# A Mamba-2 layer with a convolutional MLP: second norm's sums moved into the output projection, a chunk's own part added by TensorE, two buffers for a chunk's factors, context tiles transposed one by one

## The chip, the cores and the metric

The kernel runs on one core of a Trainium2 chip. The metric is the device time of one execution in microseconds. A core has TensorE (PE in the profile; PEld is its weight load), VectorE (DVE), ScalarE (ACT), GpSimd (POOL) and SyncE (SP). Each takes its instructions in a fixed order; in this kernel SP does nothing but issue DMAs.

## The reference

The model is one layer: a bidirectional Mamba-2 mixer and then a gated convolutional MLP, on 512 latent tokens of 1024 channels with 256 context tokens in front. Everything is float32.

```python
sh1, sc1, g1, sh2, sc2, g2 = split(silu(c) @ ada_w + ada_b, 6)     # modulation
hc, hl = modulate(rmsnorm(ctx)), modulate(rmsnorm(x))
z, xbc, dt = split(h @ w_in)                  # for context and latent tokens
xs, b, c = split(silu(conv1d(xbc, 3 taps)))   # 32 heads of 64, 4 groups, state of 128
# per direction, chunks of 128 tokens; the latent scan starts from the context's last state
y = (c b^T * decay) (dt xs)  +  decay_from_start * (c state)
x = x + g1 * (rmsnorm((y + d * xs) * silu(z)) @ w_out)
a, g = split(modulate(rmsnorm(x), sh2, sc2) @ w_up)
x = x + g2 * ((silu(conv2d(a, 3x3)) * g) @ w_down)
return rmsnorm(x)
```

## The kernel before

Products that must be exact to float32 are made of three passes: a weight tile is split into a rounded `hi` (ACT) and a rest `lo` (DVE or POOL), the activations too, and PE adds hi·hi, lo·hi and hi·lo. A raw weight tile of 512 KB comes through the pool `wraw` (three slots, line 84) and becomes a pair of the pool `wsp` (three slots, line 85). Small products, transposes and sums over partitions run on PE in plain float32.

The stages are: (1) modulation of the first norm, norm, first columns of the input projection; (2) `dt_path` (line 523), the decay factors of all heads, mostly on DVE, whose results go to DRAM (`da_d`, `em_d`, `e_d`) to be read back spread over partitions; (3) four groups of eight heads: `proj_pieces(g)` (638) projects the group's columns b, x0 to x3 and c, each with a 3-tap convolution (`conv_silu`, 629), and `ssm_group(g)` (714) runs its recurrence; (4) `gate_pieces` (822), 16 columns of z; (5) the output projection with the second norm; (6) up projection with the 3x3 convolution; (7) down projection and last norm.

`ssm_group` goes through four chunks. `mixing(ch)` (753) loads a chunk's factors: `R` (one buffer, line 759) and `M` (two) and `eb` (one). DVE scans `R` in place, adds its two directions into `M`, and multiplies `M` by `cb`. PE then makes `pi`, the chunk's own part, from `M` and the tokens `xk`, and `pe`, twice, from the states of either direction; DVE multiplies both by `eb`, adds the two, adds them to `pi`, and adds `pi` to `u` (lines 797 to 814). `pi` and both `pe` take a PSUM bank each from `py`, which has three. `advance` (745) carries a state on by one chunk. `context_states(g)` (676) transposes the context's b and x columns of the group once all five are projected, through the one bank of `pt`, and makes the first states.

The modulation's parts 2 (`g1`), 3 and 4 (second norm's shift and scale) are matrix by vector products that DVE makes: `ada_pieces` (843) loads a 512 KB tile of `ada_w` through `wraw` and adds its product with the column `s` to `ada_acc`, eight pieces per part. `ada_to_cols` (866) turns such a sum into columns with 16 small matmuls. `with_ada` (904) puts one such piece behind each piece of projection; as there are 24, they lie in the phases of groups 1 to 3 and the first gates. `blend` (931) emits the group's recurrence and after each of its eight steps so many pieces of the next phase as the ratio says (0.6, 0.6, 0.9, 0.6); the rest of the phase comes after it.

The order in which instructions are emitted is a priority. A scheduler in the compiler then sets each engine's order by its own estimate of times, except where `hold` or `T.held` pins the order to that of the program: in stage 1, and for PE from the last quarter of the output projection to the first columns of the up projection.

The output projection (`token_matmul`, 969, called at 1077) runs 16 tiles of `w_out` over four token tiles of two banks each. The first three and the last four tiles of weights are taken together, so that token tiles finish one after another; `add_and_norm` (1033) and `modulated` (1048) then make the input of the up projection in place of them, `h2hi` and `h2lo`. `gate2` (1101) makes part 5 in the up projection.

Of the kernel before, what the change touches and what calls it, by code (L numbers as in the profile page):

```python
# [10 lines left out]
F32 = mybir.dt.float32  # L11
F32R = mybir.dt.float32r
# [6 lines left out]
P = 128  # L19
# [47 lines left out]
def hybrid_kernel(  # L67
# [138 lines left out]
    gp = ph1.enter_context(tc.tile_pool(name="gp", bufs=2))  # L206
    ca = ph1.enter_context(tc.tile_pool(name="ca", bufs=1))

# [5 lines left out]
    def bank(pool, name):  # L214
        return pool.tile([P, 512], F32, tag=pool.name, name=name)
# [422 lines left out]
    def proj_pieces(g):  # L638

        def start():  # L640

            bT = gp.tile([P, LAT], F32, tag="bT", name=f"bT{g}", bufs=1)
            cT = gp.tile([P, LAT], F32, tag="cT", name=f"cT{g}")
            bTc = ca.tile([P, CTX], F32, tag="bTc", name=f"bTc{g}")
            xTc = ca.tile([P, 4, CTX], F32, tag="xTc", name=f"xTc{g}")
            grp[g] = bT, cT, bTc, xTc

        def run(raw, nm, m):
            if nm == "b":
                start()  # L650
            bT, cT, bTc, xTc = grp[g]
            if nm[0] == "x":
                i = int(nm[1])
                dl, dc = u[:, 4 * g + i], xTc[:, i]
            else:
                dl, dc = (bT, bTc) if nm == "b" else (cT, None)
            if raw is None:
                pl, pc = ps_first[nm]
            else:
                whi, wlo = split(raw, f"{nm}{g}", G if g == 0 or (g == 1 and nm in ("b", "x0", "x1", "x2")) else None)  # L660
                pc = dc is not None and project(whi, wlo, chi, clo, CTX, f"pc_{nm}{g}")
                pl = project(whi, wlo, hhi, hlo, LAT, f"pl_{nm}{g}", py if g == 0 else pj)
            if dc is not None:
                conv_silu(pc, m, CTX, dc, f"c{nm}{g}")
            conv_silu(pl, m, LAT, dl, f"l{nm}{g}")

        def finish(_):
            bT, cT, bTc, xTc = grp[g]
            grp[g] = bT, cT, context_states(g, bTc, xTc)

        for nm, m in [("b", 16 + g)] + [(f"x{i}", 4 * g + i) for i in range(4)] + [("c", 20 + g)]:
            load = partial(raw_cols, w_in, INNER + m * P, f"{nm}{g}")
            yield (None if g == 0 and nm in ps_first else load), partial(run, nm=nm, m=m)
        yield None, finish

    def context_states(g, bTc, xTc):
        bk = cx.tile([P, CTX], F32, tag="bkc", name=f"bkc{g}")
        tp = bank(pt, f"tbc{g}")
        for cc in range(2):
            T.transpose(tp[:, cc * P:(cc + 1) * P], bTc[:, cc * P:(cc + 1) * P], ident)  # L680
        A.copy(bk, tp[:, :CTX])
        S = [sp.tile([P, 512], F32, tag=f"S{dr}", name=f"S{dr}_{g}_0", bufs=(3, 4)[dr]) for dr in range(2)]
        xk = []
        for cc in range(2):
            tp = bank(pt, f"txc{g}{cc}")
            for i in range(4):
                T.transpose(tp[:, i * P:(i + 1) * P], xTc[:, i, cc * P:(cc + 1) * P], ident)
            t = cx.tile([P, 512], F32, tag=f"xkc{cc}", name=f"xkc{g}{cc}")
            A.copy(t, tp)
            xk.append(t)  # L690
        for dr in range(2):
            ps = bank(pst, f"sc{g}{dr}")
            for cc in range(2):
                local_state(ps, bk, cc, weighted(xk[cc], dr, 4 + cc, g), cc == 0, cc == 1)
            A.copy(S[dr], ps)
        return S
# [7 lines left out]
    def weighted(xk, dr, ch, g):  # L704
        t = cx.tile([P, 512], F32, tag="xw", name=f"xw{g}_{ch}_{dr}", bufs=2)
        G.tensor_tensor(
            heads(t), heads(xk),
            ej(tokcol(tok_w, dr, ch, g)), op=ALU.mult)
        return t
# [4 lines left out]
    def ssm_group(g):  # L714
# [38 lines left out]
        def mixing(ch):  # L753
# [4 lines left out]
            M = sp.tile([P, HPG, 2, BL], F32, tag="M", name=f"M{g}{ch}", bufs=2)  # L758
            R = sp.tile([P, 2, HPG, BL], F32, tag="R", name=f"R{g}{ch}", bufs=1)
            halves = [(b, slice(BL * b, BL * b + BL)) for b in range(2)]  # L760
# [36 lines left out]
        for ch in range(NC):  # L797
            cs = slice(ch * P, (ch + 1) * P)
            M, eb = nxt
            pi = bank(py, f"pi{g}{ch}").rearrange("p (j l) -> p j l", l=P)  # L800
            for j in range(4):
                for q in range(2):
                    h = 2 * j + q
                    mm(pi[64 * q:64 * q + 64, j], xk[:, ch, h * HD:(h + 1) * HD], M[:, 4 * q + j])
            t = eb
            for dr, S in ((0, Sf), (1, Sb[ch])):
                pe = bank(py, f"pe{g}{ch}{dr}").rearrange("p (j l) -> p j l", l=P)
                for j in range(4):
                    mm(pe[:, j], S[:, j * P:(j + 1) * P], cT[:, cs])
                V.tensor_tensor(pe if dr else t[:, 0], pe, eb[:, dr], op=ALU.mult)  # L810

            V.tensor_tensor(t[:, 0], t[:, 0], pe, op=ALU.add)
            V.tensor_tensor(pi, pi, t[:, 0], op=ALU.add)
            us = u[:, 4 * g:4 * g + 4, cs]
# [50 lines left out]

    def ada_to_cols(part, a):
        pc = bank(pj, f"ada_c{part}")
        for m in range(KD):
# [9 lines left out]

    def ada_to_rows(a, name):
        parts = split(a, name)  # L880
        for h in range(2):
# [22 lines left out]
    def with_ada(pieces):  # L904
        for p_ in pieces:
            yield p_
            yield from islice(ada, 1)

    ada = chain(ada_pieces(3, ada_acc, then=ada_to_cols), ada_pieces(4, ada_acc, then=ada_to_cols),
                ada_pieces(2, ada_acc, then=ada_bias))  # L910
    phases = [proj_pieces(0)] + [with_ada(p_) for p_ in (
        proj_pieces(1), proj_pieces(2), chain(proj_pieces(3), gate_pieces(0)),
        chain(gate_pieces(1), gate_pieces(2)), gate_pieces(3))] + [ada]
    ends = []
# [31 lines left out]
    finish_phase(0)  # L946
    for g, ratio in enumerate((0.6, 0.6, 0.9, 0.6)):
        blend(ssm_group(g), g + 1, ratio)
# [16 lines left out]
    h2hi = x2p.tile([P, KD, LAT], F32R, tag="h2hi", name="h2hi")  # L965
    h2lo = x2p.tile([P, KD, LAT], F32R, tag="h2lo", name="h2lo")
    Q.dma_start(x2, x.rearrange("(i p) d -> p i d", p=P))
# [49 lines left out]
    with tc.tile_pool(name="uo", bufs=5) as uo, tc.tile_pool(name="wlo", bufs=4) as wlast:  # L1017
# [11 lines left out]
        last_of = lambda: [wlast.tile([P, 1024], F32R, tag=n, name=f"{n}_last") for n in ("whi", "wlo")]  # L1029
        get_w = lambda k, last: wrows(w_out, k, f"o{k}", None, last_of if last else None)  # L1030
        xns = {}
# [45 lines left out]
        for i, o in token_matmul(acc8, 16, get_w, get_u, 3, 4, 512, up_ahead):  # L1077
            add_and_norm(i, o)
            if 0 < i < 3:
                modulated(i - 1, acc8[i - 1])  # L1080
# [20 lines left out]
    def gate2():  # L1101
        yield from stream(ada_pieces(5, g2r, True, ada_bias), 0)
        ada_to_rows(g2r, "g2b")
        yield
# [111 lines left out]
```

## Time and profile before

| | us |
|---|---|
| three timed runs | 969.15, 971.22, 972.81 |
| median | 971.22 |
| profiled execution | 972.9 |
| its span on the core | 971.1 |

| engine | busy, us | share of the span |
|---|---|---|
| PE | 902.7 | 93% |
| DVE | 717.2 | 74% |
| ACT | 344.8 | 36% |
| POOL | 301.6 | 31% |

All instructions are issued through one helper, so the profile puts them all on line 59; they are told apart by the tile that they write, as `pi` or `ada_acc`. "A <- B" after a wait names what ended it. The granted clock is the share of 2.4 GHz that TensorE had in a stretch, and its two levels are 1.2 and 2.4 GHz.

### The profile page before, as it was taken

What the parts mean: (1) busy time and instruction counts of PE and PEld (TensorE: products, weight loads), DVE (VectorE), ACT (ScalarE), POOL (GpSimd) and SP (SyncE); (2) the same over time, 40 slices, a digit from 0 to 9 for tenths busy, and PEclk for the clock granted to TensorE, in tenths of its full rate; (3) what the DMA queues carried; (4) which work ended last, traced back from release to release, by engine and by line L of the source; (5) the groups of instructions that cost most, each with busy time, mean ns of one, the idle gap of its engine ahead of it and who ended that gap; (6) DMA issues with size and microseconds to landing.
All of it is one profiled execution on the core that took longest, in us unless ns stands there. A gap on an engine that the chain in (4) does not pass through costs nothing.

```text
span 971.1 us, 12065 instructions
## 1 busy us (share of the span) xinstructions
PE 902.7 (93%) x4595; PEld 736.8 (76%) x4595; DVE 717.2 (74%) x961; ACT 344.8 (36%) x523; POOL 301.6 (31%) x223
## 2 busy tenths in 40 slices
PE   7999868788889979899999999999989999999996
PEld 6688756666667767687888888888868888888885
DVE  5689989888977889657754457878898888843336
ACT  6463332222213322334344336444544333321223
POOL 2133249454535632414100004002400000453446
PEclk9999888899999999899999999999999999999998
DMA  9923364435554365533434350334534333323322
GB/s 313 292 57 101 109 145 119 112 94 155 169 144 120 98 184 141 141 88 104 135 121 140 109 152 1 112 112 148 161 107 120 87 107 92 105 87 92 104 65 87
DMA packets 137891, 119.70 MB, mean 123 GB/s; under 512 B 23245, under 2 KB 118249, under 8 KB 137833
## 3 DMA queue, kind: packets, MB, share of 16 engines
q1 hardware_dynamic: 137833, 118.93, 42.3%
q8 instruction: 36, 0.59, 0.3%
q14 instruction: 22, 0.18, 0.1%
HBM read 116.49 MB, written 2.43 MB: 122 GB/s over the span
## 4 chain that ended last, share of the span: by engine, by line
PE 51%; DVE 24%; DMA 12%; issue 9%; POOL 2%; ACT 2%; SPq 1%; DVEq 0%; ACTq 0%; POOLq 0%
PE d L59 12%; PE o L59 8%; PE pz L59 8%; PE pg L59 7%; PE pa L59 6%; DMA R<-da_d 5%; DMA adaw<-in_ada_w_dram 4%; DVE M L59 3%; DVE ada_acc L59 3%; DVE R L59 2%; DVE et L59 2%; PE pl_x L59 2%; DVE fc L59 2%; SPq L59 1%; DVE cv_lx L59 1%
## 5 line engine op out<-in xcount | busy, mean ns | idle before, releaser
L59 DVE SCALAR_TENSOR_TENSOR fc<-pa,prmC,fc 128x441 f32<-128x441 f32 (+2 forms) x176 | 121.4, 693 | 13.3 <-ACT fc L59 9.8
L59 POOL TENSOR_TENSOR raw_d<-raw_d,g2r 128x1024 f32<-128x1024 f32 x22 | 56.1, 2556 | 176.1 <-DMA raw_d<-in_ffn_w_down_dram 159.8
L59 PE MATMUL pa<-h2lo,hi_a 128*128 128x512 f32 (+1 forms) x192 | 71.5, 373 | 0.8 <-POOL h2lo L59 0.5
L59 PE MATMUL pa<-h2hi,lo_a 128*128 128x512 f32 (+1 forms) x192 | 71.5, 372 | 0.6 <-DVE lo_a L59 0.6
L59 PE MATMUL pa<-h2hi,hi_a 128*128 128x512 f32 (+1 forms) x192 | 71.5, 373 | 0.1
L59 PE MATMUL pg<-h2hi,lo_g 128*128 128x512 f32 (+1 forms) x184 | 70.1, 381 | 0.4 <-DVE lo_g L59 0.4
L59 PE MATMUL pg<-h2hi,hi_g 128*128 128x512 f32 (+1 forms) x184 | 70.1, 381 | 0.0
L59 PE MATMUL pg<-h2lo,hi_g 128*128 128x512 f32 (+1 forms) x184 | 69.9, 380 | 0.0
L59 DVE TENSOR_TENSOR lo_d<-raw_d,hi_d 128x1024 fp32r<-128x1024 f32 x18 | 34.2, 1902 | 42.9 <-ACT hi_d L59 42.9
L59 PE MATMUL pl_x<-hhi,hi_x 128*128 128x512 f32 x128 | 54.2, 425 | 4.0 <-DVE cv_cx L59 4.0
L59 POOL TENSOR_TENSOR M<-M,tok_m 64x512 f32<-64x512 f32 x32 | 41.9, 1310 | 51.1 <-DMA M<-em_d 43.2
L59 DVE TENSOR_TENSOR_SCAN R<-R,dg 128x1024 f32<-128x1024 f32 x16 | 40.2, 2516 | 23.7 <-DMA R<-da_d 17.2
L59 PE MATMUL pl_x<-hhi,lo_x 128*128 128x512 f32 x128 | 53.4, 419 | 0.0
L59 PE MATMUL pz<-hhi,lo_z 128*128 128x512 f32 x128 | 52.7, 412 | 0.0
L59 PE MATMUL pz<-hhi,hi_z 128*128 128x512 f32 x128 | 52.7, 412 | 0.0
L59 PE MATMUL pl_x<-hlo,hi_x 128*128 128x512 f32 x128 | 51.6, 405 | 0.0
L59 PE MATMUL pz<-hlo,hi_z 128*128 128x512 f32 x128 | 51.2, 400 | 0.0
L59 POOL TENSOR_TENSOR dg<-diag,tok_dt 128x1024 f32<-128x1024 f32 x16 | 34.4, 2148 | 42.7 <-DVE R L59 41.7
L59 POOL TENSOR_TENSOR xw<-xk,tok_w 128x512 f32<-128x512 f32 x24 | 35.1, 1468 | 34.1 <-PE ps_Sf L59 17.1
L59 PE MATMUL d<-lo_d,fhi 128*128 128x512 f32 x144 | 44.5, 389 | 0.0
L59 PE MATMUL d<-hi_d,flo 128*128 128x512 f32 x144 | 44.5, 389 | 0.0
L59 PE MATMUL d<-hi_d,fhi 128*128 128x512 f32 x144 | 43.6, 389 | 0.0
(339 smaller groups left out, 2410.6 us busy)
## 6 DMA issues: line engine op xcount, KB each, us to landing
adaw<-in_ada_w_dram SPq DMA_DIRECT2D x32, 512.0 KB, 3.8
raw_a<-in_ffn_w_up_dram SPq DMA_DIRECT2D x22, 512.0 KB, 4.6
raw_g<-in_ffn_w_up_dram SPq DMA_DIRECT2D x22, 512.0 KB, 4.0
raw_d<-in_ffn_w_down_dram SPq DMA_DIRECT2D x22, 512.0 KB, 3.7
adaw<-in_ada_w_dram SPq DMA_DIRECT2D x8, 1024.0 KB
raw_x<-in_ssm_w_in_dram SPq DMA_DIRECT2D x16, 512.0 KB, 3.9
R<-da_d SPq DMA_DIRECT2D x32, 256.0 KB, 4.4
eb<-e_d SPq DMA_DIRECT2D x32, 256.0 KB, 5.1
```

The lines of the kernel that those rows point to most:

```text
L59: ins = f(*a, **kw)
```

## The change

1. Parts 3 and 4 of the modulation are summed in the output projection: each `get_w` takes one tile of `w_out` and then one piece of these parts. They have their own accumulator `ada34`, which lies under the tag of `h2lo`. Their column sums follow the second token tile and use columns of a PSUM bank of the first; `h2lo` is allocated after that. Part 2 stays in front, now behind the gate pieces of groups 1 to 3. The last blend ratio is 1.2 instead of 0.6.
2. In a chunk `pe` of the forward direction comes first; DVE multiplies it by `eb` in its PSUM bank, and the matmuls of `pi` are accumulated on it there. The product of the backward direction is written over `eb`, and one DVE instruction adds it.
3. `R` has two buffers, `xw` three.
4. Each context column is transposed and copied as soon as it is projected, from a buffer of 256 columns (two of them); `context_states` is left with the products.
5. In `gate2` the split of `g2r` is emitted a step before its matmuls.

```diff
-    ca = ph1.enter_context(tc.tile_pool(name="ca", bufs=1))
+    ca = ph1.enter_context(tc.tile_pool(name="ca", bufs=2))
...
-            if dc is not None:
+            if dk is not None:
+                dc = ca.tile([P, CTX], F32, tag="xTc", name=f"xTc{nm}{g}")
                 conv_silu(pc, m, CTX, dc, f"c{nm}{g}")
+                tp = bank(pt, f"tc{nm}{g}")
+                for cc in range(2):
+                    T.transpose(tp[:, cc * P:(cc + 1) * P], dc[:, cc * P:(cc + 1) * P], ident)
+                A.copy(dk, tp[:, :CTX].rearrange("p (c n) -> p c n", n=P))
...
-        t = cx.tile([P, 512], F32, tag="xw", name=f"xw{g}_{ch}_{dr}", bufs=2)
+        t = cx.tile([P, 512], F32, tag="xw", name=f"xw{g}_{ch}_{dr}", bufs=3)
...
-            R = sp.tile([P, 2, HPG, BL], F32, tag="R", name=f"R{g}{ch}", bufs=1)
+            R = sp.tile([P, 2, HPG, BL], F32, tag="R", name=f"R{g}{ch}", bufs=2)
...
-            pi = bank(py, f"pi{g}{ch}").rearrange("p (j l) -> p j l", l=P)
+            pes = []
+            for dr, S in ((0, Sf), (1, Sb[ch])):
+                pe = bank(py, f"pe{g}{ch}{dr}").rearrange("p (j l) -> p j l", l=P)
+                for j in range(4):
+                    mm(pe[:, j], S[:, j * P:(j + 1) * P], cT[:, cs], start=(j == 0))
+                V.tensor_tensor(eb[:, 1] if dr else pe, pe, eb[:, dr], op=ALU.mult)
+                pes.append(pe)
+            pi = pes[0]
             for j in range(4):
                 for q in range(2):
                     h = 2 * j + q
-                    mm(pi[64 * q:64 * q + 64, j], xk[:, ch, h * HD:(h + 1) * HD], M[:, 4 * q + j])
-            t = eb
-            for dr, S in ((0, Sf), (1, Sb[ch])):
-                pe = bank(py, f"pe{g}{ch}{dr}").rearrange("p (j l) -> p j l", l=P)
-                for j in range(4):
-                    mm(pe[:, j], S[:, j * P:(j + 1) * P], cT[:, cs])
-                V.tensor_tensor(pe if dr else t[:, 0], pe, eb[:, dr], op=ALU.mult)
-
-            V.tensor_tensor(t[:, 0], t[:, 0], pe, op=ALU.add)
-            V.tensor_tensor(pi, pi, t[:, 0], op=ALU.add)
+                    mm(pi[64 * q:64 * q + 64, j], xk[:, ch, h * HD:(h + 1) * HD], M[:, 4 * q + j], start=False)
+            V.tensor_tensor(pi, pi, eb[:, 1], op=ALU.add)
...
-    ada = chain(ada_pieces(3, ada_acc, then=ada_to_cols), ada_pieces(4, ada_acc, then=ada_to_cols),
-                ada_pieces(2, ada_acc, then=ada_bias))
-    phases = [proj_pieces(0)] + [with_ada(p_) for p_ in (
-        proj_pieces(1), proj_pieces(2), chain(proj_pieces(3), gate_pieces(0)),
-        chain(gate_pieces(1), gate_pieces(2)), gate_pieces(3))] + [ada]
+    ada = ada_pieces(2, ada_acc, then=ada_bias)
+    phases = [proj_pieces(0), proj_pieces(1), proj_pieces(2), chain(proj_pieces(3), gate_pieces(0)),
+              with_ada(chain(gate_pieces(1), gate_pieces(2))), with_ada(gate_pieces(3)), ada]
...
-    for g, ratio in enumerate((0.6, 0.6, 0.9, 0.6)):
+    for g, ratio in enumerate((0.6, 0.6, 0.9, 1.2)):
...
-    h2lo = x2p.tile([P, KD, LAT], F32R, tag="h2lo", name="h2lo")
+    ada34 = x2p.tile([P, 4, D], F32, tag="h2lo", name="ada34")
...
-        get_w = lambda k, last: wrows(w_out, k, f"o{k}", None, last_of if last else None)
+        mod2 = stream(chain(ada_pieces(3, ada34[:, 0]), ada_pieces(4, ada34[:, 1])), 0)
+
+        def get_w(k, last):
+            w = wrows(w_out, k, f"o{k}", None, last_of if last else None)
+            next(mod2, None)
+            return w
...
             add_and_norm(i, o)
+            if i == 1:
+                for part in (3, 4):
+                    ada_to_cols(part, ada34[:, part - 3], acc8[0][1][:, 32 * part:])
+                h2lo = x2p.tile([P, KD, LAT], F32R, tag="h2lo", name="h2lo")
...
-        ada_to_rows(g2r, "g2b")
+        parts = split(g2r, "g2b")
+        yield
+        ada_to_rows(g2r, "g2b", parts)
         yield
```

## Rows read from the trace of the kernel before

**Rows 1.** The page: busy engines, and what the DMAs moved in 40 slices
```profile
PE 902.7 (93%) x4595; PEld 736.8 (76%) x4595; DVE 717.2 (74%) x961; ACT 344.8 (36%) x523; POOL 301.6 (31%) x223
...
GB/s 313 292 57 101 109 145 119 112 94 155 169 144 120 98 184 141 141 88 104 135 121 140 109 152 1 112 112 148 161 107 120 87 107 92 105 87 92 104 65 87
```

**Rows 2.** Table by stretches: length, busy time (x instructions) by engine, granted clock, DMA
```profile
core 0: us, PE busy (x) PEld busy (x) DVE busy (x) ACT busy (x) POOL busy (x), PEclk, DMA share, GB/s
...
64.00:137.00 73.00, 65.66 (x354) 56.89 (x353) 67.70 (x110) 29.74 (x51) 22.85 (x24) 0.93 0.38 102
137.00:305.00 168.00, 137.84 (x790) 108.56 (x790) 143.12 (x142) 43.80 (x72) 93.83 (x62) 0.92 0.51 140
305.00:353.00 48.00, 45.78 (x270) 36.27 (x270) 38.57 (x41) 15.97 (x27) 27.23 (x19) 1.00 0.41 117
353.00:440.00 87.00, 78.44 (x386) 61.45 (x386) 59.80 (x74) 27.48 (x43) 25.91 (x19) 0.92 0.49 124
...
503.00:588.00 85.00, 84.89 (x382) 70.02 (x381) 41.51 (x59) 34.99 (x52) 4.07 (x4) 1.00 0.45 140
...
645.00:708.00 63.00, 63.00 (x279) 52.19 (x279) 52.31 (x69) 28.53 (x35) 17.60 (x7) 1.00 0.51 150
```

**Rows 3.** Chain of waits, 64 to 440 us: its shares by engine or transfer
```profile
by line: DMA R<-da_d 13.4%; PE pz L59 7.7%; DVE M L59 7.7%; issue 7.0%; DVE ada_acc L59 6.9%; DVE R L59 5.9%; DMA adaw<-in_ada_w_dram 5.5%; DVE et L59 5.4%; PE pl_x L59 3.5%; DVE cv_lx L59 3.0%; SPq L59 2.9%; DMA M<-em_d 2.4%; PE sc L59 2.0
```

**Rows 4.** Timelines of DVE and SP: start, length, instruction
```profile
215.57 3.48 DVE L59 TENSOR_TENSOR M<-R 64x512 f32<-64x512 f32 x2
...
219.07 0.57 SPq L59 DMA_DIRECT2D R<-da_d  x1
219.80 1.22 SPq L59 DMA_DIRECT2D eb<-e_d  x2
```

**Rows 5.** Tile `ada_acc`: PE, PEld, DVE, ACT busy by stretches; duration min/median/max in ns
```profile
64.00:137.00 73.00, 0.00 (x0) 0.00 (x0) 10.23 (x6) 0.00 (x0) 0.93 0.38 102
137.00:440.00 303.00, 3.91 (x32) 4.28 (x32) 33.94 (x26) 0.00 (x0) 0.93 0.49 132
...
L59 DVE SCALAR_TENSOR_TENSOR ada_acc<-adaw,s_col,ada_acc x21: 1250/1627/3518, 84.1 to 370.9; 128x1024 f32<-128x1024 f32 x21
```

**Rows 6.** Tile `raw_o`, instructions and landing; chain of waits, one column of 24 matmuls
```profile
L59 ACT CAST hi_o<-raw_o x12: 1038/1039/1052, 498.5 to 556.6; 128x1024 fp32r<-128x1024 f32 x12
L59 DVE TENSOR_TENSOR lo_o<-raw_o,hi_o x12: 1217/1226/1229, 499.6 to 557.9; 128x1024 fp32r<-128x1024 f32 x12
...
DMA to landing us min/median/max: 3.4/4.8/6.1
...
734.72 5.44 PE pa L59 x24
```

**Rows 7.** Tile `eb`: the add of the two directions, and the landing of its loads
```profile
L59 DVE TENSOR_TENSOR eb<-eb,pe x16: 654/680/689, 186.4 to 486.0; 128x512 f32<-128x512 f32 x16
...
DMA to landing us min/median/max: 4.4/5.1/6.5
```

**Rows 8.** Waits of PE, 64 to 440 us: total us, times, longest
```profile
PE pi L59 <- DVE M L59: 8.8, 2, 6.9
PE pe L59 <- DVE u L59: 8.0, 4, 4.0
...
PE pi L59 <- DVE eb L59: 4.4, 2, 3.3
PE pl_x L59 <- DVE cv_cx L59: 4.0, 2, 3.8
...
PE pe L59 <- DVE eb L59: 2.9, 3, 1.8
...
PE tok_t L59 <- DVE tok_w L59: 1.6, 1, 1.6
```

**Rows 9.** Waits of DVE, 64 to 500 us: total us, times, longest
```profile
DVE eb L59 <- DMA eb<-e_d: 7.9, 5, 1.9
```

**Rows 10.** Timeline of PE in the up projection
```profile
713.53 0.50 PE L59 MATMUL g2b<-lo_g2b,ones_sq 128*128 128x512 f32 x1 [1.85 <-DVE lo_g2b L59]
```

More of the change, by code (lines that the diff above doesn't have):

```diff
@@ L643, in start @@
             cT = gp.tile([P, LAT], F32, tag="cT", name=f"cT{g}")
-            bTc = ca.tile([P, CTX], F32, tag="bTc", name=f"bTc{g}")
-            xTc = ca.tile([P, 4, CTX], F32, tag="xTc", name=f"xTc{g}")
-            grp[g] = bT, cT, bTc, xTc
+            bkc = cx.tile([P, 1, CTX], F32, tag="bkc", name=f"bkc{g}")
+            xkc = cx.tile([P, 2, 512], F32, tag="xkc", name=f"xkc{g}")
+            grp[g] = bT, cT, bkc, xkc
         def run(raw, nm, m):
@@ L650, in run @@
                 start()
-            bT, cT, bTc, xTc = grp[g]
+            bT, cT, bkc, xkc = grp[g]
             if nm[0] == "x":
                 i = int(nm[1])
-                dl, dc = u[:, 4 * g + i], xTc[:, i]
+                dl, dk = u[:, 4 * g + i], xkc[:, :, i * P:(i + 1) * P]
             else:
-                dl, dc = (bT, bTc) if nm == "b" else (cT, None)
+                dl, dk = (bT, bkc.rearrange("p a (c n) -> p (a c) n", n=P)) if nm == "b" else (cT, None)
             if raw is None:
@@ L660, in run @@
                 whi, wlo = split(raw, f"{nm}{g}", G if g == 0 or (g == 1 and nm in ("b", "x0", "x1", "x2")) else None)
-                pc = dc is not None and project(whi, wlo, chi, clo, CTX, f"pc_{nm}{g}")
+                pc = dk is not None and project(whi, wlo, chi, clo, CTX, f"pc_{nm}{g}")
                 pl = project(whi, wlo, hhi, hlo, LAT, f"pl_{nm}{g}", py if g == 0 else pj)
-            if dc is not None:
+            if dk is not None:
+                dc = ca.tile([P, CTX], F32, tag="xTc", name=f"xTc{nm}{g}")
                 conv_silu(pc, m, CTX, dc, f"c{nm}{g}")
+                tp = bank(pt, f"tc{nm}{g}")
+                for cc in range(2):
+                    T.transpose(tp[:, cc * P:(cc + 1) * P], dc[:, cc * P:(cc + 1) * P], ident)
+                A.copy(dk, tp[:, :CTX].rearrange("p (c n) -> p c n", n=P))
             conv_silu(pl, m, LAT, dl, f"l{nm}{g}")
         def finish(_):
-            bT, cT, bTc, xTc = grp[g]
-            grp[g] = bT, cT, context_states(g, bTc, xTc)
+            bT, cT, bkc, xkc = grp[g]
+            grp[g] = bT, cT, context_states(g, bkc[:, 0], xkc)
         for nm, m in [("b", 16 + g)] + [(f"x{i}", 4 * g + i) for i in range(4)] + [("c", 20 + g)]:
@@ L674, in proj_pieces, with context_states @@
         yield None, finish
[L676 to L681, printed above, removed]
-        S = [sp.tile([P, 512], F32, tag=f"S{dr}", name=f"S{dr}_{g}_0", bufs=(3, 4)[dr]) for dr in range(2)]
[L683 to L690, printed above, removed]
+    def context_states(g, bk, xk):
+        S = [sp.tile([P, 512], F32, tag=f"S{dr}", name=f"S{dr}_{g}_0", bufs=(3, 4)[dr]) for dr in range(2)]
         for dr in range(2):
@@ L693, in context_states @@
             for cc in range(2):
-                local_state(ps, bk, cc, weighted(xk[cc], dr, 4 + cc, g), cc == 0, cc == 1)
+                local_state(ps, bk, cc, weighted(xk[:, cc], dr, 4 + cc, g), cc == 0, cc == 1)
             A.copy(S[dr], ps)
@@ L864, in ada_pieces, with ada_to_cols @@
             yield partial(load, k), partial(run, k=k)
-    def ada_to_cols(part, a):
-        pc = bank(pj, f"ada_c{part}")
+    def ada_to_cols(part, a, pc):
         for m in range(KD):
@@ L877, in ada_bias, with ada_to_rows @@
             V.scalar_tensor_tensor(a[:, s], ident, prmB[:, KD * part + m:KD * part + m + 1], a[:, s], ALU.mult, ALU.add)
-    def ada_to_rows(a, name):
-        parts = split(a, name)
+    def ada_to_rows(a, name, parts=None):
+        parts = parts or split(a, name)
         for h in range(2):
```

## The prediction

> **What bounds the kernel now.** I read the page first [rows 1]: TensorE (PE) is busy for 93% of the span and VectorE (DVE) for 74%, so PE is the engine to follow, and the question is where it isn't fed. The table by stretches answers that [rows 2]. In the output projection (503 to 588 us) PE is busy for 84.89 of 85 us at full clock, and DVE has 43 us to spare. From 64 to 440 us, with the recurrence, PE stands idle for 73 - 65.66 = 7.3, 168 - 137.84 = 30.2, 48 - 45.78 = 2.2 and 87 - 78.44 = 8.6 us, 48.3 us in all. There its granted clock is 0.93, 0.92, 1.00 and 0.92, a mix of the two levels 2.4 and 1.2 GHz; the missing shares of 73, 168 and 87 us are 5.1 + 13.4 + 7.0 = 25.5 us. So the stretch loses 73.8 us of PE time, and no edit there can give more.
>
> The reason is on DVE: 67.70 + 143.12 + 38.57 + 59.80 = 309.2 of 376 us busy [rows 2], in one queue that serves the recurrence, the convolutions, the weight splits and the modulation sums. The chain of waits of the stretch [rows 3] runs for 13.4% (50 us) through transfers of `R`, 6.9% (26 us) through the sums `ada_acc`, 5.5% (21 us) through their weights `adaw`; PE's own shares are small. The timeline shows the `R` loop [rows 4]: DVE reads `R` until 215.57 + 3.48 = 219.05, and the next half of `R` is issued at 219.07. With a single buffer the transfer waits for the reader each time.
>
> **The change part by part.**
>
> *Sums of the second norm's shift and scale (parts 3 and 4).* 16 of 24 pieces leave the stretch for the output projection; the other 8 (part 2, with its bias) move to the last two gate phases. The stretch sheds 10.23 + 33.94 = 44.2 us of DVE [rows 5], 14% of its load. A piece takes 1.63 us there in the median and up to 3.5, against 1.25 at best [rows 5]. Before 137 us six pieces lie in the chain of the decay factors, which is mostly DVE work, so the first `R` can be loaded up to 10 us earlier. In the output projection 16 pieces at 1.25 cost DVE 20.0 us: 41.5 + 20.0 = 61.5 of 85 us, beside PE.
>
> What could show there is the loads. Each step then takes two tiles through the three `wraw` slots in 24 matmuls, 5.44 us [rows 6], so a slot has 8.2 us per tile. A weight tile needs 4.8 us to land in the median, 1.04 for its `hi`, 1.23 for its `lo` [rows 6]: 7.1 us; a modulation tile 4.8 + 1.25 = 6.1. That fits by 1 us; with the slowest landing, 6.1, the weight tile needs 8.4 and doesn't. By bytes: 140 GB/s x 85 us = 11.9 MB [rows 2] plus 8.4 MB makes 239 GB/s, under the 313 of the page's first slice [rows 1]. The nearest row for such a mix is the up projection from 645 to 708 us, where the loads of part 5 pass the same slots: PE is busy for 63.00 of 63 us [rows 2]. The worst place is the start: `ada34` seems to lie in the space of the projections' inputs, so the first piece would hold its slot until the last gate matmul, and the 2 MB of `x` go out just then. Bounds 0 to 10 us; I take 2, nearest to the up projection's row.
>
> *The column sums (`ada_to_cols`).* Their matmuls, 3.91 us of PE [rows 5], move behind the second token tile of the output projection, in PE's fixed order. If the stretch becomes PE bound they cost nothing net; if it stays bound by DVE they cost 3.9: I take 2. Behind them wait the transposes of the first normalized tile, for two short DVE instructions.
>
> *Two buffers for `R`.* The transfer can go while the former `R` is still scanned. An `R` issued earlier stands on SP's queue before `eb` and `M`, in an order fixed at build time. The 50 us of chain don't come back as such: behind them stand `eb` (still one buffer), DVE's queue and PE's own work.
>
> *Own part added on TensorE.* Per chunk DVE loses one add of 0.68 us [rows 7]; with three of four groups, 12 chunks, in the stretch that is 8.2 us. A chunk needs two of the three `py` banks instead of three, so the waits of PE for a bank that DVE still reads should go: 8.0 (`pe` <- `u`) + 4.4 (`pi` <- `eb`) + 2.9 (`pe` <- `eb`) = 15.3 us [rows 8]. New is that the `pi` matmuls wait for DVE's first product, thus for the landing of `eb`; behind them PE's whole queue waits, projections included. Bounds: 0 where the scheduler has put projections in front, 16 x (5.1 us landing + 0.68 us product) = 92 us where all of it is exposed [rows 7]. Nearest is what DVE waits for `eb` now, 7.9 us in 5 of 16 chunks [rows 9]: I take 7.9 us.
>
> *Context tiles one by one, `xw` with three buffers, blend ratios, `g2b`.* The transposes stay ten per group; ACT gets two more copies per group, and is busy for 29.7 + 43.8 + 16.0 + 27.5 = 117 of 376 us there [rows 2]: nothing, and if that cover were gone, eight instructions of about the 0.68 us of [rows 7], 5 us. With the sums out of the way, more projection pieces fall between the recurrence's steps; this is how the gain below is reached, and I give it no term of its own. In the up projection the matmuls of `g2b` come a step after their split: PE's wait of 1.85 us [rows 10] goes. Bounds 0 to 3, I take 2.
>
> *Sum.* Of PE's waits in the stretch [rows 8]: banks 15.3; the 4.0 us of `pl_x` for `cv_cx`, an instruction of DVE's crowded queue; and of the seven other causes on DVE or GpSimd (8.8 down to 1.6, 27.8 us together) half, 13.9, since DVE sheds 44.2 + 8.2 = 52.4 of 309 us and the `R` transfer leaves their chain. That is 33.2. Of the 25.5 us of clock, all lost in stretches where PE idles, half: 12.7. Less the new wait: 33.2 + 12.7 - 7.9 = 38.0 us. Less 2 + 2 in the output projection, plus 2 at `g2b`: 36 us. The profiled run took 972.9 us (971.1 span and 1.8 around it), so 936.9; it lies 1.7 above the median of the three timed runs, and I forecast 936.
>
> **The rivals.**
> 1. *DVE's chain only gets a new link.* `eb` keeps one buffer and each chunk still goes transfer, product, matmul, add; waits on `M`, `Sb` and `xw` stay. Then only banks, `cv_cx` and a quarter of the clock come back: 15.3 + 4.0 + 6.4 - 7.9 - 2 = 16 us, 957. For it: DVE waits for `eb` already [rows 9]. Against: the `eb` loop is about 5.1 landing, 3 x 0.68 on DVE and the matmuls, some 9 us, where 376 us hold 12 chunks.
> 2. *The stretch becomes PE bound.* The chain sheds 50 + 26 + 21 = 97 us, more than the 73.8 that PE can give; in 305 to 353 us PE idles only 2.2 us of 48 at full clock with DVE at 80%. If five sixths of the loss go: 62 - 2 = 60 us, 913.
> 3. *Transfers in line.* `eb` is issued right behind a half of `R` at 219.80 already [rows 4], and over all chunks `eb` lands in 4.4 to 6.5 us [rows 7], so little delay shows. With the 2 MB of `x` among them the weight tiles land in 3.4 to 6.1 us [rows 6], 2.7 us at most for it; `R`, 0.5 MB, is a quarter of that, 0.7 us per chunk, 11 us if all of it is exposed: 947. The Trainium skill (DMA: Bandwidth & Descriptors, Queues, rings and completion order) says that each DMA engine takes descriptors in ring order, by which an early `R` delays the `eb` behind it. By that rule the time is this rival's; the landings of `eb` bear it out weakly.
> 4. *Slower: TensorE's queue stops for `eb`.* If `pi` stands right behind its `pe` in PE's order, PE stalls for landing and product. Gain and loss balance at (36 + 7.9) / 16 = 2.7 us per chunk; at 3.5 us, 56 us in place of 7.9: 985. For it: PE is in order, and `eb` is reloaded only after the former chunk's last add. Against: four `pe` of the second direction lie between, and DVE finds `eb` landed in 11 of 16 chunks [rows 9].
> 5. *It doesn't do what it says.* The order on SP and DVE is fixed at build time; `R` may still be issued late, while the denser blend delays the recurrence: gains and losses cancel, 972.
>
> **How the numbers follow.** Forecast 0.50 (its own range 920 to 950), rivals 1 to 5: 0.20, 0.12, 0.05, 0.08, 0.05. Faster by over 0.5% (4.9 us, about what a measurement of this kernel can tell from no change) are the forecast and rivals 1 to 3: 0.87; same 0.05; slower 0.08. The range 908 to 962 leaves out rivals 4 and 5 (0.13) and the outer half of rival 2 (0.06).
>
> **What would show it.** Right: PE's idle time and missing clock between 64 us and the end of the recurrence near 35 us instead of 74; no DVE wait for `R`; no PE wait for `u` or `eb` as a bank's reader; sums in the output projection at 1.25 us each with PE still full there; the `R` loop no longer tied to its reader. Wrong: a wait of `pi` for the product of over 2 us per chunk; a PE wait for `lo_o` at the start or end of the output projection; the last `u` of the recurrence later than the last gate.

## The result, and the profile after

The changed kernel takes 981.18 us in the median (978.86 to 982.95), the kernel before took 970.52 beside it: a ratio of 1.0106, with a 95% interval of 1.0076 to 1.0136. It is slower by 10 us, where 36 us less were forecast. The profiled execution of after took 978.86 us with a span of 977.1, that of before 972.9 with 971.1, so the two traces show 6.0 of the 10 us. The sums below go by these two spans.

The page of after, busy engines and what the DMAs moved in 40 slices, answers [rows 1]:

```profile
PE 907.7 (93%) x4595; PEld 740.3 (76%) x4595; DVE 700.6 (72%) x945; ACT 347.8 (36%) x531; POOL 301.7 (31%) x223
...
GB/s 316 285 65 47 56 155 74 76 121 124 95 127 77 98 118 141 183 139 119 87 227 225 207 160 1 109 108 152 160 97 130 87 95 99 106 88 87 108 64 87
```

DVE has 16 instructions and 17 us less; slices 21 to 23, the output projection, now carry 207 to 227 GB/s. The table by stretches, with the columns of [rows 2]:

```profile
64.00:137.00 73.00, 64.01 (x354) 54.37 (x352) 59.78 (x102) 31.81 (x55) 26.23 (x28) 0.95 0.37 86
137.00:305.00 168.00, 146.86 (x843) 115.48 (x844) 131.80 (x133) 48.24 (x82) 99.71 (x66) 0.94 0.39 104
305.00:353.00 48.00, 43.90 (x248) 36.80 (x248) 32.02 (x39) 17.64 (x30) 18.11 (x13) 0.96 0.27 72
353.00:440.00 87.00, 80.55 (x402) 62.55 (x401) 65.14 (x73) 27.32 (x41) 34.48 (x25) 0.96 0.56 157
503.00:588.00 85.00, 76.19 (x332) 62.96 (x332) 53.94 (x66) 28.16 (x39) 2.52 (x2) 0.93 0.62 193
```

Read as in the prediction, PE idles from 64 to 440 us for 9.0 + 21.1 + 4.1 + 6.5 = 40.7 us (48.3 before), and the clock takes 3.7 + 10.1 + 1.9 + 3.5 = 19.2 (25.5 before). So 59.9 us of PE time are lost there in place of 73.8: 14 us came back, not 38. The last gate matmul ends at 492.3 us, before at 503.4: the front gained 11.1. (The 14 us and the 3.9 of the column sums that left the stretch don't all show there: 4.0 went into first matmuls of the output projection ahead of the last gates, and from 440 to 492 us PE lost 2.7 by idling and 1.6 by its clock. That leaves 9.6; the other 1.5 of the 11.1 isn't accounted for.)

The output projection gives that back and more. The next table cuts it where TensorE begins with the last four tiles of weights; first the kernel before, then after, with the same columns:

```profile
503.40:570.40 67.00, 67.00 (x301) 55.61 (x300) 30.59 (x36) 28.37 (x35) 0.00 (x0) 1.00 0.52 161
570.40:595.00 24.60, 23.98 (x115) 19.65 (x113) 17.44 (x35) 10.68 (x28) 8.63 (x7) 1.00 0.13 37
```

```profile
492.30:559.40 67.10, 66.07 (x292) 53.57 (x291) 40.54 (x46) 25.15 (x32) 0.00 (x0) 1.00 0.71 229
559.40:600.30 40.90, 33.05 (x147) 27.87 (x145) 25.27 (x47) 14.81 (x32) 8.19 (x7) 0.83 0.37 114
```

The first twelve tiles take 67 us in both. The last four take 40.9 us in place of 24.6: 16.3 more, of which 3.9 are the column sums [rows 5], 7.85 - 0.62 = 7.2 more idle time, and the remaining 5.2 the lower clock, 0.83. What follows the output projection differs by 0.7 us. The account of the spans: -11.1 + 0.1 + 16.3 + 0.7 = +6.0.

Where PE stops there is seen in its timeline (start, length, instruction, and in brackets the idle time before it and what ended it), with DVE's below it:

```profile
571.91 0.61 PE L59 MATMUL o<-whi_last,ul 128*128 128x512 f32 x2
575.84 3.57 PE L59 MATMUL o<-ones,ada 128*128 128x1 f32 x16 [3.31 <-DVE ot L59]
582.46 3.58 PE L59 MATMUL o<-ones,ada 128*128 128x1 f32 x16 [3.04 <-DVE modc L59]
...
569.00 1.23 DVE L59 TENSOR_TENSOR lo_a<-raw_a,hi_a 128x1024 fp32r<-128x1024 f32 x1 [1.97 <-ACT hi_a L59]
571.67 1.23 DVE L59 TENSOR_TENSOR lo_g<-raw_g,hi_g 128x1024 fp32r<-128x1024 f32 x1 [1.44 <-ACT hi_g L59]
573.24 1.22 DVE L59 TENSOR_TENSOR lo_a<-raw_a,hi_a 128x1024 fp32r<-128x1024 f32 x1 [0.35 <-ACT hi_a L59]
574.38 1.40 DVE L59 SCALAR_TENSOR_TENSOR ot<-o,rstd,ada_acc 128x512 f32<-128x512 f32 x2
```

The column sums write into a bank of token tile 0, so they wait until `ot` has read it; part 4's, in the same bank, wait again until DVE has read part 3's (`modc`). `ot` stands in DVE's queue behind three splits of up weights (`lo_a`, `lo_g`, `lo_a`), and these wait for weights whose loads come out of the same three slots after all 32 tiles of this stage. The first up weight is issued at 563.2 us here, 3.8 us after the last weights' first matmul; before it was issued at 559.1, 11.3 us ahead of it.

The waits of PE from 64 to 440 us (total, times, longest), against [rows 8]:

```profile
PE pe L59 <- DVE pe L59: 10.3, 3, 5.7
PE ps_Sb L59 <- POOL xw L59: 7.5, 4, 2.9
PE ps_Sb L59 <- DVE Sb L59: 6.5, 2, 5.2
PE sc L59 <- POOL xw L59: 5.3, 1, 5.3
PE tcx L59 <- ACT xTcx L59: 2.9, 3, 1.5
PE tx L59 <- ACT u L59: 2.3, 1, 2.3
PE tok_t L59 <- DVE ww L59: 2.2, 1, 2.2
PE tok_t L59 <- DVE tok_w L59: 2.1, 1, 2.1
```

The waits for a bank (15.3 us) and for `cv_cx` (4.0) are gone, and the new wait for the product, the first line, is 10.3. The other lines sum to 28.8 us, with three shorter ones that aren't shown to 30.2: the causes changed names, their sum didn't fall below the 27.8 of before. The chain of waits of the stretch, against [rows 3], has `R` at 16.4% of its shares, not less than 13.4%:

```profile
by line: DMA R<-da_d 16.4%; issue 7.3%; DVE M L59 7.1%; DVE et L59 6.2%; PE pl_x L59 4.8%; DVE R L59 4.7%; PE pz L59 4.0%; SPq L59 3.8%; PE pe L59 3.5%; POOL xw L59 2.9%; PE pc_x L59 2.8%; PE pl_c L59 2.8%; DMA eb<-e_d 2.4%; DVE cv_lx L59 2
```

So there are two questions: what starves the end of the output projection, and why `R` is still waited for although it has two buffers.

### The profile page after: what moved, and what is told of

The parts are those of the page before. It is cut to its first block, busy times and chain, and to the rows that moved or that the text cites. A ratio compares the mean times of both kernels' runs of the same rounds, so it can differ in the third digit from the quotient of the medians.

```text
span 977.1 us, 12057 instructions
## 1 busy us (share of the span) xinstructions
PE 907.7 (93%) x4595; PEld 740.3 (76%) x4595; DVE 700.6 (72%) x945; ACT 347.8 (36%) x531; POOL 301.7 (31%) x223
## 4 chain that ended last, share of the span: by engine, by line
PE 50%; DVE 22%; DMA 14%; issue 4%; POOL 3%; ACT 3%; SPq 2%; DVEq 0%; ACTq 0%; POOLq 0%
PE d L59 12%; PE pg L59 11%; PE pa L59 10%; DMA R<-da_d 6%; PE pz L59 4%; DMA adaw<-in_ada_w_dram 3%; DMA raw_o<-in_ssm_w_out_dram 3%; DVE M L59 3%; DVE et L59 2%; PE pe L59 2%; PE pl_x L59 2%; SPq L59 2%; DVE R L59 2%; PE o L59 2%; DVE fc L59 1%
## 5 line engine op out<-in xcount | busy, mean ns | idle before, releaser
L59 POOL TENSOR_TENSOR x<-x,ot 128x512 f32<-128x512 f32 x4 | 5.1, 1276 | 124.0 <-DVE ot L59 121.4
```

What stands on the lines that cost most here:

```text
L59: ins = f(*a, **kw)
```

## The experiments

**The two halves of the change.** First one half alone, then the other, both on the kernel before. e1 has the sums, the phases and the ratio:

```diff
-    for g, ratio in enumerate((0.6, 0.6, 0.9, 0.6)):
+    for g, ratio in enumerate((0.6, 0.6, 0.9, 1.2)):
...
+            w = wrows(w_out, k, f"o{k}", None, last_of if last else None)
+            next(mod2, None)
```

> Only the sums of parts 3 and 4 move into the output projection (with the phases, the last blend ratio and the column sums that belong to it); the recurrence is that of before. Theory (the gain in front is given back in the output projection, which loses some 24 us: 3.9 of column sums, 11 of idle PE, 9 of clock): front shorter by 10 us, output projection longer by 24, about 984. Rival (the recurrence's edits are what costs, the sums are cheap where they went): 965 or less.

Measured: 974.05 us, 1.0045 (1.0031 to 1.0060). The gates end at 487.4 us, 16.0 earlier than before, but the output projection at 595.6, after 108.2 us in place of 91.6. The time lies between the two forecasts.

e2 has the recurrence alone:

```diff
-            R = sp.tile([P, 2, HPG, BL], F32, tag="R", name=f"R{g}{ch}", bufs=1)
+            R = sp.tile([P, 2, HPG, BL], F32, tag="R", name=f"R{g}{ch}", bufs=2)
...
+                V.tensor_tensor(eb[:, 1] if dr else pe, pe, eb[:, dr], op=ALU.mult)
+                pes.append(pe)
```

> Only the recurrence's edits: own part on TensorE, two buffers for R, three for xw, context tiles one by one; the sums stay in front. Theory: PE no longer waits for py banks, 15 us of its waits go and 8 to 10 come back at the product, so 960 to 968. Rival (the wait of pi for the product and the transfers that now stand behind eb cost more than they give): 975 to 985.

Measured: 968.97 us, 1.0002 (0.9984 to 1.0020). Alone, the recurrence's edits are worth nothing, which neither forecast had; the sums cost, and the loss is in the output projection.

The two halves don't simply add up. The changed kernel has e1's sums too, yet it is slower than e1 (1.0106 against 1.0045; the intervals don't meet), and in the traces its gates end 4.9 us later, at 492.3 against 487.4 us, while the output projection takes 108 us in both. So beside the moved sums the other edits cost some 6 us. Taking back `R`'s second buffer or the own part doesn't help (e7 and e8 below, both on e4). The context tiles and the third buffer of `xw` were not run by themselves, so which edit costs this stays open.

**What starves the output projection.** e3 lets the column sums wait a token tile longer, with the transposes of the first two token tiles behind them, and part 4 uses another bank:

```diff
-            if i == 1:
+            if i == 2:
...
-                    ada_to_cols(part, ada34[:, part - 3], acc8[0][1][:, 32 * part:])
+                    ada_to_cols(part, ada34[:, part - 3], acc8[0][part - 3][:, 32 * part:])
...
-            if 0 < i < 3:
-                modulated(i - 1, acc8[i - 1])
+                for j in range(2):
+                    modulated(j, acc8[j])
```

> The changed kernel, with the column sums and the transposes of the first two token tiles behind the third token tile, and a bank for each part. Theory: in the changed kernel PE waits there 3.3 us for DVE's read of the bank and 3.0 us for the first part's add, and its clock then falls to 0.54 for 15 us (7 us); without these waits about 10 us less than the changed kernel, 971. Rival (PE waits there anyway, for the late weights): within 3 us of the changed kernel, 978 to 983.

Measured: 977.63 us, 1.0079 (1.0052 to 1.0106). It gives back some 3 us, and PE then stops 5.9 us for `modc`; a later place alone doesn't remove the stop.

e4 leaves the order as it is and gives the modulation's tiles of this stage two slots of their own:

```diff
-        mod2 = stream(chain(ada_pieces(3, ada34[:, 0]), ada_pieces(4, ada34[:, 1])), 0)
+        mod2 = stream(chain(ada_pieces(3, ada34[:, 0], pool=adq), ada_pieces(4, ada34[:, 1], pool=adq)), 0)
```

> The changed kernel, with two slots of their own for the 16 tiles of the moved sums, so that the weights have the three of wraw to themselves. Theory (slots, not bytes, make the last weights late): the last tile of w_out is split by 558 instead of 564.6, the weights of the up projection are split before DVE has to read the first token tile; about 10 us less than the changed kernel, 971. Rival (the bytes are the bound, 193 GB/s in this stage and 243 at its end): 978 to 983.

Measured: 970.98 us, 1.0010 (0.9991 to 1.0029). The same two stretches of the output projection:

```profile
495.40:561.00 65.60, 65.53 (x292) 53.71 (x292) 47.03 (x51) 27.96 (x35) 0.00 (x0) 1.00 0.75 259
561.00:592.50 31.50, 30.58 (x147) 26.13 (x145) 18.99 (x42) 11.13 (x29) 8.20 (x7) 0.89 0.22 62
```

The last four tiles take 31.5 us, 9.4 less than in after, and PE idles 0.9 in place of 7.85. The same bytes, more of them per us (259 GB/s against 229), land in time. It was the three slots, not the bandwidth and not DVE's sums. e4 takes back 10.2 us and is level with the kernel before. Its last four tiles still take 6.9 us more than there, of which 3.9 are the column sums.

**Whether `R`'s transfers hold the front.** e5, on e4, loads `R` once and keeps it (30 of 32 loads are left out), with the scan writing another tile:

```diff
-            R = sp.tile([P, 2, HPG, BL], F32, tag="R", name=f"R{g}{ch}", bufs=2)
+            if not kept:
+                kept.append(sp.tile([P, 2, HPG, BL], F32, tag="R", name="R", bufs=1))
...
+            R = sp.tile([P, 2, HPG, BL], F32, tag="Rs", name=f"Rs{g}{ch}", bufs=1)
```

> Built on the kernel with own slots (e4, 971). R is loaded once and kept; the other 30 of its 32 loads, and with them the right factors of all chunks but the first, are left out; the scan writes into a tile of its own. Theory (R's transfers, 60 us of the chain of 64 to 440 us also with two buffers, hold back the recurrence and through it PE): 15 us or more less than e4, 956 or below. Rival (other things stand right behind R: loads of M and eb, GpSimd's xw, the states' chain; R's loads on the chain are only the last of several to come): within 5 us of e4, 966 to 976.

Measured: 949.87 us, 0.9810 (0.9788 to 0.9831), 21 us below e4. The transfers do hold the front.

e6 issues them from another queue, e7 takes the second buffer away again, both on e4:

```diff
-                Q.dma_start(
+                A.dma_start(
                     R[r].rearrange("p d h l -> p d (h l)"),
```

> The kernel with own slots (e4), with R's loads issued by ACT instead of SP, so that they don't stand behind the load of eb, which waits for the former chunk's last add. Theory (the second buffer is idle because R is issued behind eb on SP): DVE's waits for R (17 us) go, 8 us or more less than e4, 963 or below. Rival (as for e5): within 5 us of e4.

Measured: 970.03 us, 1.0001 (0.9974 to 1.0028). In e6 every load but the first ones leaves within 0.04 us of the end of the add into `M` that reads the buffer; in e4 it left up to 1.8 us behind that add. So SP's order held the loads back little, and what they wait for is the add.

```diff
-            R = sp.tile([P, 2, HPG, BL], F32, tag="R", name=f"R{g}{ch}", bufs=2)
+            R = sp.tile([P, 2, HPG, BL], F32, tag="R", name=f"R{g}{ch}", bufs=1)
```

> The kernel with own slots (e4), with one buffer for R as before. Theory (the second buffer gains nothing where R is issued behind eb): within 4 us of e4, 967 to 975. Rival (as forecast: the buffer takes transfers off the chain): 8 us or more above e4, 979 or above.

Measured: 972.02 us, 1.0039 (1.0017 to 1.0062). The second buffer is worth 1.0 us by the medians and 2.8 by the ratios; the two intervals overlap.

**The own part.** e8 makes `pi` as before, in a bank of its own, on e4:

```diff
+            pi = bank(py, f"pi{g}{ch}").rearrange("p (j l) -> p j l", l=P)
...
+            V.tensor_tensor(t[:, 0], t[:, 0], pe, op=ALU.add)
+            V.tensor_tensor(pi, pi, t[:, 0], op=ALU.add)
```

> The kernel with own slots (e4), with the chunk's own part in a bank of its own and added by DVE as before: pi doesn't wait for a product, DVE has one add more per chunk, a chunk takes three banks of py. Theory (gain of the banks and cost of the product's wait cancel): within 4 us of e4, 967 to 975. Rival 1 (as forecast, the banks are worth more than the wait): 5 us or more above e4. Rival 2 (the wait for the product, 10 us of PE's waits in the changed kernel, costs more than it gives): 5 us or more below e4.

Measured: 974.56 us, 1.0066 (1.0043 to 1.0089). The own part on TensorE is worth 3.6 us by the medians, 5.4 by the ratios.

**What `R` waits for.** The timelines of after, DVE and then SP, show how one chunk of the recurrence follows another:

```profile
169.38 2.62 DVE L59 TENSOR_TENSOR_SCAN R<-R,dg 128x1024 f32<-128x1024 f32 x1
...
192.22 0.69 DVE L59 TENSOR_TENSOR pe<-pe,eb 128x512 f32<-128x512 f32 x1
192.82 1.38 DVE L59 TENSOR_TENSOR M<-R 64x512 f32<-64x512 f32 x2
196.03 0.68 DVE L59 TENSOR_TENSOR u<-u,pe 128x512 f32<-128x512 f32 x1
...
205.25 2.65 DVE L59 TENSOR_TENSOR M<-R 64x512 f32<-64x512 f32 x2
213.54 2.29 DVE L59 TENSOR_TENSOR_SCAN R<-R,dg 128x1024 f32<-128x1024 f32 x1 [1.70 <-DMA R<-da_d]
...
192.03 1.25 SPq L59 DMA_DIRECT2D M<-em_d  x2
193.45 1.96 SPq L59 DMA_DIRECT2D eb<-e_d  x2
195.51 1.22 SPq L59 DMA_DIRECT2D R<-da_d  x2
207.93 1.23 SPq L59 DMA_DIRECT2D R<-da_d  x2
```

The scan writes `R` in place, so a buffer is not free when the scan has read it but when the result has been added into `M` (192.82 and 205.25), and that add needs a free `M`, which PE gives back once per chunk (the load of `M`'s other half, which needs the same buffer, goes at 192.03, when PE's own-part matmuls have ended at 191.95). The next `R` is issued right after the add (195.51, 207.93), and the scan of it stands near the start of DVE's next chunk, where DVE waits for the landing. A second buffer doesn't loosen this: it holds a scanned `R` that waits for `M`, not one that is landing. The `R` scanned at 169.38 us is added only at 205.25. Theory M was that `M`'s two buffers are the cause; its rivals were the single buffer of `eb` (E), the scan's place in DVE's order (O) and SP's order (Q).

e9 is e7 with three buffers for `M`, e10 is e7 with two for `eb`:

```diff
-            M = sp.tile([P, HPG, 2, BL], F32, tag="M", name=f"M{g}{ch}", bufs=2)
+            M = sp.tile([P, HPG, 2, BL], F32, tag="M", name=f"M{g}{ch}", bufs=3)
```

> e7 (own slots, one buffer for R) with three buffers for the mixing matrix M. In the traces so far R's next load is issued within 1 to 2 us after DVE has added a scanned R into its M, and that add stands behind the load of M's other half, which waits until TensorE has read the M of two chunks before. Theory M (M's two buffers hold R back): with a third M the add comes a chunk earlier, R's loads go out earlier, DVE's wait for R (20 to 25 us in e4 and e6) falls by at least half, and the time comes out 6 to 15 us below e7's 972.0, at 957 to 966. Rival E (the one buffer of eb and its load in the chunk's own chain set the pace): within 2 us of e7, 970 to 974, and R's wait only turns into one for eb. Rival O (the scan's place in DVE's order is the cause): 970 to 974 as well, with R issued earlier but waited for as long.

Measured: 976.85 us, 1.0071 (1.0044 to 1.0098).

```diff
-            eb = sp.tile([P, 2, 4, P], F32, tag="eb", name=f"eb{g}{ch}", bufs=1)
+            eb = sp.tile([P, 2, 4, P], F32, tag="eb", name=f"eb{g}{ch}", bufs=2)
```

> e7 with two buffers for eb, so that the load of the next chunk's factors no longer waits for DVE's last add of the chunk before. Theory M: no gain above 3 us, 969 to 974, since R still waits for M. Rival E: the wait of DVE's products for eb (15.8 us in after) goes and the time falls by 8 to 15 us, to 957 to 964. Rival O: 969 to 973.

Measured: 974.49 us, 1.0058 (1.0038 to 1.0078). Neither gains, so neither number of buffers is the cause, and theory M in that form falls. In e10 DVE's wait for `eb` is gone (16.4 us in e7), but its wait for `R` grew from 30.2 to 35.4, so E falls too. e9 comes out 4.8 us above e7, which no reading had forecast; the intervals overlap. In e9 the add and the load stand as they did (DVE, then SP):

```profile
195.33 1.38 DVE L59 TENSOR_TENSOR M<-R 64x512 f32<-64x512 f32 x2
...
197.51 1.25 SPq L59 DMA_DIRECT2D R<-da_d  x2
```

The third `M` is filled once, by an add at 170.81 us where e7 has none until 192.07, and is then as full as two were: in the steady state the add still comes once per chunk, when PE gives a buffer back, and the load still starts behind it.

e11 cuts the link itself. It is e4 with `R`'s two buffers put to different use, one for the load and one for the scan's result:

```diff
-            R = sp.tile([P, 2, HPG, BL], F32, tag="R", name=f"R{g}{ch}", bufs=2)
+            R = sp.tile([P, 2, HPG, BL], F32, tag="R", name=f"R{g}{ch}", bufs=1)
+            Rs = sp.tile([P, 2, HPG, BL], F32, tag="Rs", name=f"Rs{g}{ch}", bufs=1)
...
-            scan(flat, flat, dg.rearrange("p d h l -> p (d h l)"))
+            scan(Rs.rearrange("p d h l -> p (d h l)"), R.rearrange("p d h l -> p (d h l)"), dg.rearrange("p d h l -> p (d h l)"))
...
-                V.tensor_tensor(M[r, :, b], R[r, 0], R[r, 1, :, ::-1], op=ALU.add)
+                V.tensor_tensor(M[r, :, b], Rs[r, 0], Rs[r, 1, :, ::-1], op=ALU.add)
```

> e4 with R's two buffers used differently: one that the load fills, and one that the scan writes, so that the load of the next chunk waits only for the scan and not for the add into M. Theory M: the next R is on its way while the scanned one waits for M, so its landing is hidden and the time comes out 5 to 15 us below e4's 971.0, at 956 to 966. Rival E: 969 to 972, no gain. A fourth reading, Q (the load stands in the issuing queue behind eb's, which waits for DVE): 968 to 972 here, and a gain of 5 us or more only in the next run.

Measured: 950.89 us, 0.9804 (0.9779 to 0.9830): as fast as e5, which leaves the loads out, and 20.1 us below e4, more than the 5 to 15 of theory M. DVE and SP in e11:

```profile
195.55 2.55 DVE L59 TENSOR_TENSOR_SCAN Rs<-R,dg 128x1024 f32<-128x1024 f32 x1
203.77 1.38 DVE L59 TENSOR_TENSOR M<-Rs 64x512 f32<-64x512 f32 x2
205.78 2.28 DVE L59 TENSOR_TENSOR_SCAN Rs<-R,dg 128x1024 f32<-128x1024 f32 x1
...
198.13 1.22 SPq L59 DMA_DIRECT2D R<-da_d  x2
```

The load goes at 198.13, when the scan has read the former `R` (195.55 + 2.55 = 198.10), and 7.7 us later the next scan starts without a wait. The tile's own list of waits has 0.7 us for the landing of `R`, against 25.5 us in e4:

```profile
  DMA R<-da_d: 0.7, 1
```

e12 is e11 with the loads on ACT's queue (e6's edit):

> e11 with R's loads issued by ScalarE's queue in place of SP's, so that they are not behind the loads of eb and M. Theory M: as e11 within 3 us. Reading Q: 5 to 15 us below e11, since the scan frees R and nothing else holds it in this queue. Rival E: 969 to 972, as e4 and e6.

Measured: 951.57 us, 0.9823 (0.9788 to 0.9858). Reading Q falls. Reading O had no run of its own; against it stands that in e11 the scan still stands between two adds in DVE's order (203.77 and 215.28 us) and no longer waits.

**Whether this holds in the changed kernel itself.** The same edit as in e11, in after (three shared slots) and in e2:

> The changed kernel with e11's one edit: R is loaded into one buffer and the scan writes another, so that the load waits for the scan and not for the add into M; the output projection's loads share three slots as in after. If R's buffer is a cause of its own, the 20.1 us of e11 against e4 come off after's 981.2: 961, within 957 to 965. If the three slots of the output projection take a faster front's gain away again, 968 to 975.

Measured: 961.39 us, 0.9924 (0.9897 to 0.9951), 19.8 us below after. The gates end at 474.5 us and the output projection takes 108.1, as in after: the two causes add up.

> e2 (the recurrence edits alone) with the same edit. If R's buffer is a cause of its own, 20 us below e2's 969.0: 949, within 945 to 953, and as fast as e11, so that the second norm's sums are worth nothing even with slots of their own. If the gain needs the sums' work moved out of the front, 955 to 963; if the front is held by the projections' column sums here, 965 to 969.

Measured: 958.30 us, 0.9894 (0.9852 to 0.9936), 10.7 below e2 and 7.4 above e11. `R`'s buffer is a cause of its own, but without the sums' move it gives less (half by the medians; the four times of e14 spread over 8.7 us): the gates end at 486.4 us, against 475.1 in e11. So the sums' move is worth having once its loads have slots of their own and `R`'s link is cut.

e15 is e11 with e3's edit:

> e11 with e3's edit too (the modulation's columns a token tile later, part 4 in another bank). If the wait for the columns still stops TensorE at the end of the output projection, 3 to 4 us below e11's 950.9, at 947 to 948; if the own slots have taken that wait away, 950 to 952.

Measured: 948.76 us, 0.9779 (0.9742 to 0.9815). The interval covers e11's ratio, so whether the 2 us are real is open. e11 and e15 are faster than the kernel before by 2% and than the changed kernel by 3%.

## Why the prediction was wrong

Between the 36 us less of the forecast and the 6.0 us more of the two traces lie 42 us. The front gained 11.1 where 38.0 were forecast, which is 26.9 of them; the output projection lost 16.4 where 4 were forecast, 12.4; and what follows lost 0.7 where 2 were to be gained, 2.7, for which no run shows the reason.

*What bounds the kernel: right.* The `R` loop through its reader was the chain of the stretch: without that link (e5, e11) the time falls by 21 and 20 us.

*The step that failed first: "Two buffers for `R`. The transfer can go while the former `R` is still scanned."* The buffer's reader isn't the scan but the add into `M`, which [rows 4] itself shows: `M<-R` ends at 219.05 and `R` is issued at 219.07. The right row was read, and the wrong life of the buffer was concluded from it. The edit is worth 1 to 3 us (e7). From it hung two terms: half of the other waits (13.9; they were 27.8 us before and are 30.2) and half of the clock (12.7; 6.3 came back). With the link cut, the step holds to its mechanism: in e11 the stretch loses 28.1 idle + 13.9 clock = 42.0 us, where the prediction wanted "near 35".

*A term mis-sized beside it: the 44.2 us of sums that leave the stretch.* It counted all 24 pieces. The eight of part 2 still ran inside the stretch, from 368.8 us on, and with their bias take 13.7 us of DVE there (the table of `ada_acc` in after, DVE first):

```profile
64.00:440.00 376.00, 13.71 (x16) 0.00 (x0) 0.95 0.41 109
```

So 30.5 us of sums left, not 44.2.

*The second failed step: the loads of the output projection, sized at 2 within 0 to 10.* The last four tiles' stretch alone grew by 16.3 us, or 12.4 without the column sums. The sum divided the slots' time by 16 steps of 5.44 us, 8.2 us per tile. But the last four tiles are taken together, and nothing of TensorE's work covers their loads except the twelve steps ahead of them. Four of the 32 tiles were issued before 493 us, and the other 28 had 67.1 us in three slots: 67.1 x 3 / 28 = 7.2 us per tile. They took (560.6 - 493.1) x 3 / 27 = 7.5. The last weight tile was issued at 559.2 and split at 564.6 us, 5 us after its group's first matmul. The slots were too few on average, not only with the slowest landing, and the up weights behind them came later still. The up projection was a poor nearest row, for its weights aren't collected by four. The worst place that was named, the start, showed as well. The first sum into `ada34` waited 6.3 us for the last gate matmul, as supposed, and the `raw_o` that is issued at 493.15 us, 0.8 us behind the 2 MB of `x`, took the longest to land (9.3 us against 6.1 of [rows 6]):

```profile
DMA to landing us min/median/max: 4.0/4.3/9.3
```

*The column sums: 2 forecast, more measured.* Their matmuls moved as described, but stand after a stop of 3 us each, at a low clock, and take 3.57 + 3.58 = 7.15 us in place of 3.91 [rows 5]. "Behind them wait the transposes" was seen; what they themselves wait for, `ot` behind DVE's splits, was not.

*What held.* The bank waits and `cv_cx` are gone (19.3 us). The first `R` was loaded 6.3 us earlier (125.1 us against 131.4), forecast up to 10. The product wait is 10.3 us against 7.9; in e5, with DVE no longer held by `R`, PE's line for it has 0.9 us, in e11 3.0, so most of this wait was `R`'s too. The sums in the output projection take 1.28 us each, forecast 1.25:

```profile
L59 DVE SCALAR_TENSOR_TENSOR ada<-adaw,s_col,ada x14: 1277/1283/1286, 493.6 to 565.7; 128x1024 f32<-128x1024 f32 x14
```

The wait of [rows 10] is gone; `g2b`'s second matmul follows its first at once:

```profile
718.80 0.39 PE L59 MATMUL g2b<-hi_g2b,ones_sq 128*128 128x512 f32 x1
719.03 0.39 PE L59 MATMUL g2b<-lo_g2b,ones_sq 128*128 128x512 f32 x1
```

*The rivals.* Rival 1 (a new link in DVE's chain, 957) names the front best: DVE waits for `eb` for 15.8 us in after, 7.9 before [rows 9], and for `R` as well. But the link that held was the old one, `R` (a second `eb` gains nothing, e10), and the rival priced the output projection at 2 too. Rival 3, the transfers in line, isn't it: e6 and e12 move `R`'s loads to another queue and the time by 1.0 and 0.7 us, and in after `eb` lands in 4.5 us in the median, no later than the 5.1 of [rows 7]. Rival 4 landed near the time (985) by a mechanism that didn't happen: PE's product wait grew by 2.4 us over the forecast, not by 48. Of the signs of being wrong, the wait for `lo_o` came true in small: 1.0 us at the start, and 0.5 for its counterpart `wlo_last` at the end. The stops that cost, 6.3 us for `ot` and `modc`, were not among the signs.

## What to carry to other kernels

A second buffer hides a load only if the consumer of the *loaded* data frees it; where an operation works in place, the buffer lives until the result has been used, and here a second buffer only held a second result. Ask of each buffer which instruction is its last reader, and give the in-place result a tile of its own first (20 us here, for no more memory). When loads are added to a stage that shares slots, divide the time by the steps that come before the first use of the last group, not by all steps, and follow what is queued in those slots behind it.

## What was not expected of the hardware

The granted clock was 0.54 from 575 to 590 us in after, close to the lower level of 1.2 GHz (0.50), although TensorE was at work for 11.1 of the 15 us; it had stopped 3.3 us before, and the work was in large part 32 one-column matmuls. In e4, where these matmuls ran from 571.6 to 576.7 us and no stop is longer than 0.9 us, it was still 0.77 over the same 15 us, with TensorE busy throughout; in before, with other matmuls at this place, 1.00. The rows of after, and below them of e4:

```profile
575.00:590.00 15.00, 11.12 (x48) 10.57 (x49) 9.67 (x25) 5.36 (x15) 2.66 (x3) 0.54 0.21 58
```

```profile
575.00:590.00 15.00, 15.00 (x68) 12.93 (x69) 6.75 (x20) 5.67 (x16) 3.81 (x3) 0.77 0.01 2
```

That the queue of a load makes so little difference wasn't expected either, by e6's theory at least: in e6 and e12 the 32 loads of 256 KB go over a second queue, 8.39 MB by their pages, and the time stays within 1 us of e4's and e11's. The Trainium skill (DMA: Bandwidth & Descriptors, Queues, rings and completion order) has rings of its own for each queue. So the ring order that the prediction's third rival spoke of has no price that these runs show.
